# Selecting the top keys in other passes, and one gate projection seven heads later

## The chip, the cores and the metric

The kernel runs on one core of a Trainium2 chip. The metric is the device time of one execution, from launch to the last write, in microseconds (us). TensorE (PE in the rows; PEld is its weight load) does the matrix products, VectorE (DVE) and ScalarE (ACT) the element work, GpSimd (POOL) some of it, and SyncE (SP) issues most transfers.

## The reference, cut to what matters

One decoder block over 1024 positions and 1024 channels. Eight heads of forgetting attention (the fox heads, 0 to 7) and eight heads of sparse attention (the DSA heads, 8 to 15) run on projections of the same normed input; two gates, sigmoids of 1024 projected columns each, weigh the two branches; then come an output projection and an MLP.

```python
iscore = jnp.where(causal[None], iscore, -jnp.inf)
_, sel = lax.top_k(iscore, topk)              # 256 keys per query, one list for all DSA heads
...
merged = (jax.nn.sigmoid(gate_fox) * (y_fox @ w_branch_fox)
          + jax.nn.sigmoid(gate_dsa) * (y_dsa @ w_branch_dsa))
```

The list of 256 keys depends on an index score that is shared by all DSA heads. Ties are broken in favour of the earlier key.

## The kernel before, in words

The queries lie in eight tiles of 128. For tiles 2 to 7 (those with more than 256 admissible keys) the kernel finds the 256th largest score of each query by bisection on its 32 bits, 16 high bits first (`Thi`), then 16 low bits (`Tlo`). One step of `bisect_step` counts, for each query, the keys at or above a candidate: tiles 2 to 5 on VectorE (line 487), tiles 6 and 7 on ScalarE with a sign function and its accumulator (line 484); line 507 takes both counts. Afterwards `select_tile(i)` turns the threshold into a mask: `sel[i]` becomes 0 for a chosen key and 1e30 for the others, W = (i+1)*128 columns wide, so 384 to 1024. `sel[i]` holds the low bits of those keys whose high bits equal the threshold, until then. `bjunk` and `eqt` are one buffer each, so the six tiles take turns in them.

The masks are read first by head 8, the first DSA head, in line 552, behind line 551, which adds a position bias and runs for DSA heads alone.

The heads run in a Python loop. Each turn issues the attention of head n, the q and k projection of head n+1 (`proj_qk`), every second time a v projection, and the gate projections that the table `GC` gives to this turn (`gate_tile`). All these projections go through `gemm_h`: 24 products per half, two halves, in the two PSUM banks of tile `g`, which rotate. A bank is free again when ScalarE and VectorE have copied it out: lines 308 to 314 for q and k (the last VectorE reads are lines 310 and 314), line 598 for a gate. Their weights come through a ring of three staging tiles `st` and two pairs `whi`, `wlo`, so they keep the order of the program among themselves.

In the same turns, four bisection steps are issued behind each fox head, and the six `select_tile` calls behind head 7. The framework then orders the instructions of each engine by a list schedule, and each engine runs its own list strictly in order. The schedule pulls the bisection and the selection forward: in the trace the selection runs beside head 5. In attention, line 552 adds the mask and takes the row minimum from PSUM tile `S`, line 556 is the exponential, line 559 scales by the reciprocal of the sum (558), and lines 573 and 574 split the transposed weights into `ph` and `pl` for the product with V.

Of the kernel before, what the change touches and what calls it, by code (L numbers as in the profile page):

```python
# [16 lines left out]
AF = mybir.ActivationFunctionType  # L17
ALU = mybir.AluOpType
# [14 lines left out]
BIG = 1.0e30  # L33
# [24 lines left out]
def block_kernel(ctx: ExitStack, tc: tile.TileContext, x, c, w_ada, b_ada, g_norm1, w_in, b_forget,  # L58
                 rel_bias, w_bf, w_bd, w_out, g_norm2, w_mlp1, w_mlp2, g_final, onehot, out):
    nc = tc.nc  # L60
# [47 lines left out]
    def split_w(pieces, lo_eng=None, kt=KT, dst=None):  # L108
        st = stg.tile([P, 1024], F32, name="st", tag="st")
        view = st.rearrange("p (k c) -> p k c", k=kt)  # L110
        for d0, d1, src in pieces:
            nc.sync.dma_start(view[:, :, d0:d1], src)
        return split_st(st, lo_eng, dst)
# [47 lines left out]
    isc, sel = [None, None], [None, None]  # L161
# [293 lines left out]
    cnt = pA.tile([P, NQ], F32, name="cnt")  # L455
    goal = pA.tile([P, NQ], F32, name="goal")
    nct = pA.tile([P, NQ], F32, name="nct")
# [52 lines left out]
    def select_tile(i):  # L510
        q, W = i - 2, (i + 1) * P
        hi = isc[i].bitcast(I16)[:, 1::2]
        L = sel[i].bitcast(U16)
        th, tl, nd = Thi[:, q:q + 1], Tlo[:, q:q + 1], need[:, q:q + 1]
        gt, eq = bjunk[:, :W], eqt[:, :W]
        nc.vector.tensor_scalar(gt, L, tl, None, op0=ALU.is_gt, op1=ALU.add, accum_out=cnt[:, q:q + 1])
        nc.vector.tensor_tensor(nd, nd, cnt[:, q:q + 1], op=ALU.subtract)
        nc.vector.tensor_scalar(eq, L, tl, None, op0=ALU.is_equal)
        nc.vector.scalar_tensor_tensor(gt, hi, th, gt, op0=ALU.is_gt, op1=ALU.add)
        nc.vector.scalar_tensor_tensor(eq, hi, th, eq, op0=ALU.is_equal, op1=ALU.mult)  # L520
        nc.vector.tensor_tensor_scan(out=L, data0=eq, data1=eq, initial=0.0, op0=ALU.add, op1=ALU.max)
        nc.vector.scalar_tensor_tensor(eq, L, nd, eq, op0=ALU.is_le, op1=ALU.mult)
        nc.vector.tensor_tensor(gt, gt, eq, op=ALU.add)
        nc.vector.tensor_scalar(sel[i], gt, -BIG, BIG, op0=ALU.mult, op1=ALU.add)


    def attention(kind, h, qk, V, Yd=None):
# [164 lines left out]

    heads = [(k, h) for k in range(2) for h in range(NH)]
    yd_stack, wo_stack = ExitStack(), ExitStack()
    GC = (2, 2, 2, 1, 1, 1, 1, 1, 1, 1, 1, 1, 1)
    GATES, g0 = {}, 0
    for n, w in enumerate(GC):
        GATES[n] = tuple(range(g0, g0 + w))
# [19 lines left out]
    for n, (kind, h) in enumerate(heads):  # L718
# [18 lines left out]
        if n == NH - 1:  # L737
            for i in range(2, NTT):
                select_tile(i)
# [22 lines left out]
    for cp in range(4):  # L762
        hi, lo = split_w([(0, 256, wbv[1][:, :, cp * 256:cp * 256 + 256])], nc.gpsimd, 4)
        hv, lv = hi.rearrange("p (k c) -> p k c", k=4), lo.rearrange("p (k c) -> p k c", k=4)
        for c2 in range(2):
            ct, cs = 2 * cp + c2, slice(c2 * P, c2 * P + P)
            for half in range(2):
                sl = slice(half * 512, half * 512 + 512)
                gt = pY.tile([P, 512], F32, name="gt2", tag="gt2", bufs=3)
# [22 lines left out]
    with ExitStack() as st4:  # L792
# [6 lines left out]
        for ch in range(2):  # L799
# [3 lines left out]
            for t in range(NTT):  # L803
                hf, tl = t // 4, slice((t % 4) * P, (t % 4) * P + P)
# [398 lines left out]
```

## Time and profile before

| | us |
|---|---|
| median of 3 runs | 1657.38 |
| lowest and highest | 1656.96, 1659.05 |
| the profiled execution | 1664.09 |
| its span, first to last instruction | 1662.3 |
| busy: PE, DVE, ACT, POOL | 1582.9, 1155.4, 955.7, 684.4 |
| mean granted TensorE clock | 0.976 |

The rows further down come from the one profiled execution. Times there are counted from the start of its span. A granted clock of 1.00 is 2.4 GHz, of 0.50 it is 1.2 GHz; a mean between them is a stretch that had both. The seven stretches of 198 to 535 are cut at the first exponential of each head: head 1 begins at 198, head 2 at 243, head 7 at 503, and head 8 at 535.

### The profile page before, as it was taken

Reading aid. Unit: us, or ns where it says so; the run is one execution under the profiler, and the core shown is the slowest. Engines: PE = TensorE matmul, PEld = TensorE weight load, DVE = VectorE, ACT = ScalarE, POOL = GpSimd, SP = SyncE. Lnnn points to the kernel's source line nnn. Section 1 sums busy time; section 2 is a strip of 40 time slices with the busy share of each in tenths; the row PEclk is TensorE's granted clock in tenths of the full one; section 3 lists DMA queues with packets and bytes.
Section 4 is the critical chain, followed back from the end, with each engine's and each line's share of the span. In section 5 each row is a group of like instructions: output and inputs, shape, how many; then the busy total and the mean of one; then the engine's idle time right before and its main releaser. Section 6 shows DMA issues by size and latency. Waiting matters only on the chain.

```text
span 1662.3 us, 22793 instructions
## 1 busy us (share of the span) xinstructions
PE 1582.9 (95%) x7585; PEld 1310.5 (79%) x7585; DVE 1155.4 (70%) x2293; ACT 955.7 (57%) x1674; POOL 684.4 (41%) x569
## 2 busy tenths in 40 slices
PE   5989999998989999999999998999999989999998
PEld 3767787786778888888887787888888868888887
DVE  6786999999954556556666535866565464758987
ACT  4366997898566777677753135554555343533433
POOL 3421121221123574756643211677776544334730
PEclk8999999998999999999999999999999989999999
DMA  9221122222232443444876435554444469665862
GB/s 299 77 59 51 50 74 55 52 66 49 74 77 67 125 133 106 131 143 139 287 257 230 151 121 194 168 185 160 154 147 158 178 240 361 230 212 188 281 209 102
DMA packets 221757, 250.92 MB, mean 151 GB/s; under 512 B 49072, under 2 KB 134144, under 8 KB 221640
## 3 DMA queue, kind: packets, MB, share of 16 engines
q1 hardware_dynamic: 215304, 235.83, 44.8%
q10 hardware_dynamic: 6336, 13.63, 2.1%
q8 instruction: 60, 0.98, 0.2%
q14 instruction: 57, 0.47, 0.1%
HBM read 184.38 MB, written 65.03 MB: 150 GB/s over the span
## 4 chain that ended last, share of the span: by engine, by line
PE 74%; DVE 14%; ACT 4%; DMA 4%; issue 3%; POOL 1%; SPq 1%; DVEq 0%; ACTq 0%; POOLq 0%
PE g L75 33%; PE S L75 23%; PE tr L75 8%; PE pv L75 7%; DVE bjunk L487 3%; PE ptr L572 2%; DVE acc L247 1%; DMA gt<-G_d 1%; DVE pl L574 1%; DVE sp L552 1%; DMA wap<-in_w_ada_dram 1%; ACT eqt L484 1%; ACT sp L556 1%; DVE gt L777 1%; ACT sp L559 1%
## 5 line engine op out<-in xcount | busy, mean ns | idle before, releaser
L75 PE MATMUL g<-h_hi,whi 128*128 128x512 f32 x656 | 266.5, 406 | 8.8 <-DVE KA L314 6.4
L75 PE MATMUL g<-h_hi,wlo 128*128 128x512 f32 x656 | 263.9, 402 | 0.0
L75 PE MATMUL g<-h_lo,whi 128*128 128x512 f32 x656 | 263.0, 401 | 0.0
L118 POOL TENSOR_TENSOR wlo<-st,whi 128x1024 fp32r<-128x1024 f32 x56 | 137.3, 2453 | 293.9 <-ACT whi L117 265.4
L1026 DVE TENSOR_TENSOR ut<-rw,ut 128x1024 fp32r<-128x1024 f32 x112 | 179.0, 1644 | 69.5 <-ACT ut L1025 69.5
L1025 ACT ACTIVATE ut<-rw 128x1024 fp32r<-128x1024 f32 x112 | 112.0, 1052 | 144.9 <-PE pv L75 66.5
L1040 POOL TENSOR_TENSOR rw<-rw 128x1024 f32<-128x1024 f32 x40 | 115.6, 2893 | 127.3 <-DMA rw<-in_w_mlp_dram 110.0
L75 PEld LDWEIGHTS g<-h_hi,whi 128*128 128x128 f32 x656 | 126.2, 192 | 34.8 <-DVE KA L314 4.3
L75 PEld LDWEIGHTS g<-h_hi,wlo 128*128 128x128 f32 x656 | 125.6, 191 | 24.7
L75 PEld LDWEIGHTS g<-h_lo,whi 128*128 128x128 f32 x656 | 125.8, 192 | 23.6
L75 PE MATMUL S<-ut 128*128 128x512 f32 (+1 forms) x576 | 138.2, 384 | 0.0
L75 PEld LDWEIGHTS S<-ut 128*128 128x128 f32 x576 | 106.5, 190 | 21.5 <-DVE ut L1026 0.4
L574 DVE TENSOR_TENSOR pl<-ptr,ph 128x512 fp32r<-128x512 f32 (+1 forms) x160 | 99.5, 630 | 27.2 <-ACT ph L573 23.5
L573 ACT ACTIVATE ph<-ptr 128x512 fp32r<-128x512 f32 (+1 forms) x160 | 86.1, 551 | 55.4 <-PE ptr L572 51.2
L556 ACT ACTIVATE sp<-sp,mn 128x128 f32<-128x128 f32 (+7 forms) x128 | 98.5, 771 | 28.3 <-DVE mn L552 28.1
L117 ACT ACTIVATE whi<-st 128x1024 fp32r<-128x1024 f32 x70 | 73.8, 1054 | 65.9 <-PE g L75 23.1
L487 DVE TENSOR_SCALAR_CACHE_REDUCE bjunk<-sel_all,cand 128x384 bf16<-128x384 int16 (+7 forms) x132 | 106.3, 806 | 1.4
L559 ACT ACTIVATE sp<-sp,mn 128x128 f32<-128x128 f32 (+7 forms) x128 | 96.8, 770 | 17.2 <-DVE mn L558 16.7
L75 PE MATMUL g<-ut 128*128 128x512 f32 (+1 forms) x384 | 94.7, 382 | 6.1 <-ACT ut L1025 4.6
L572 PE MATMUL ptr<-ident,sp 128*128 128x128 f32 x576 | 91.2, 274 | 9.8 <-DVE pl L574 9.8
L75 PE MATMUL pv<-ph,V 128*128 128x256 f32 x320 | 86.8, 291 | 1.6 <-DVE yt L581 0.9
L75 PEld LDWEIGHTS g<-ut 128*128 128x128 f32 x384 | 69.9, 191 | 21.0 <-ACT ut L1025 5.0
(433 smaller groups left out, 3883.4 us busy)
## 6 DMA issues: line engine op xcount, KB each, us to landing
rw<-in_w_mlp_dram SPq DMA_DIRECT2D x72, 512.0 KB
rw<-U_d SPq DMA_DIRECT2D x56, 512.0 KB
wap<-in_w_ada_dram SPq DMA_DIRECT2D x64, 256.0 KB
st<-in_w_mlp_dram SPq DMA_DIRECT2D x32, 512.0 KB
st<-in_w_in_dram SPq DMA_DIRECT2D x26, 512.0 KB
U_d<-cc SPq DMA_DIRECT2D x48, 256.0 KB
st<-in_w_in_dram SPq DMA_DIRECT2D x33, 256.0 KB
G_d<-t SPq DMA_DIRECT2D x32, 256.0 KB
```

What stands on the lines that cost most here:

```text
L75: nc.tensor.matmul(o, l, r, start=start, stop=stop)
L117: nc.scalar.activation(hi, st, AF.Copy)
L118: (lo_eng or nc.vector).tensor_tensor(lo, st, hi.bitcast(F32), op=ALU.subtract)
L487: nc.vector.tensor_scalar(bjunk[:, :(i + 1) * P], sel[i].bitcast(dt), thr[:, q], None, op0=ALU.is_ge, op1=ALU.add, accum_out=cnt[:, q])
L556: nc.scalar.activation(sp[:, :W], sp[:, :W], AF.Exp, bias=mn[:, len(cs) - 1:len(cs)], scale=-1.0, accum_out=mn[:, 2:3])
L559: nc.scalar.activation(sp[:, :W], sp[:, :W], AF.Copy, scale=mn[:, 3:4])
L572: nc.tensor.transpose(tr[:, n * P:(n + 1) * P], pt[s][:, kb * P:(kb + 1) * P], ident)
L573: nc.scalar.activation(ph[:, z:], tr[:, z:], AF.Copy)
L574: nc.vector.tensor_tensor(pl[:, z:], tr[:, z:], ph[:, z:].bitcast(F32), op=ALU.subtract)
L1025: nc.scalar.activation(ut[:, n], t, AF.Copy)
L1026: nc.vector.tensor_tensor(ut[:, n + 1], t, ut[:, n].bitcast(F32), op=ALU.subtract)
L1040: nc.gpsimd.tensor_tensor(o, a, b, op=op)
```

## The change

Two edits. In `select_tile`, the count of keys above the threshold moves from a VectorE pass with accumulator to a ScalarE sign pass with accumulator, whose result is +1 or -1 (so `cnt` is twice the number less W, which two one-column instructions make good); the sum `gt + eq` and the final scaling are replaced by one VectorE pass that gives 0 for chosen and 1 for other keys, and a ScalarE copy that scales it by 1e30. And in the table of gates, turn 1 issues one gate projection in place of two, and turn 7 two in place of one; the gates between keep their order, so each turn from 2 to 6 does the gate of one number lower.

```diff
--- before.py
+++ after.py
@@ -513,15 +513,18 @@
         L = sel[i].bitcast(U16)
         th, tl, nd = Thi[:, q:q + 1], Tlo[:, q:q + 1], need[:, q:q + 1]
         gt, eq = bjunk[:, :W], eqt[:, :W]
-        nc.vector.tensor_scalar(gt, L, tl, None, op0=ALU.is_gt, op1=ALU.add, accum_out=cnt[:, q:q + 1])
-        nc.vector.tensor_tensor(nd, nd, cnt[:, q:q + 1], op=ALU.subtract)
+        nt, nw = nct[:, q:q + 1], goal[:, q:q + 1]
+        nc.vector.tensor_scalar(nt, tl, -1.0, -0.5, op0=ALU.mult, op1=ALU.add)
+        nc.vector.tensor_scalar(nw, nd, float(W // 2), None, op0=ALU.subtract)
+        nc.scalar.activation(gt, L, AF.Sign, bias=nt, accum_out=cnt[:, q:q + 1])
         nc.vector.tensor_scalar(eq, L, tl, None, op0=ALU.is_equal)
-        nc.vector.scalar_tensor_tensor(gt, hi, th, gt, op0=ALU.is_gt, op1=ALU.add)
         nc.vector.scalar_tensor_tensor(eq, hi, th, eq, op0=ALU.is_equal, op1=ALU.mult)
         nc.vector.tensor_tensor_scan(out=L, data0=eq, data1=eq, initial=0.0, op0=ALU.add, op1=ALU.max)
+        nc.vector.scalar_tensor_tensor(nd, cnt[:, q:q + 1], -0.5, nw, op0=ALU.mult, op1=ALU.add)
+        nc.vector.scalar_tensor_tensor(gt, hi, th, gt, op0=ALU.is_gt, op1=ALU.add)
         nc.vector.scalar_tensor_tensor(eq, L, nd, eq, op0=ALU.is_le, op1=ALU.mult)
-        nc.vector.tensor_tensor(gt, gt, eq, op=ALU.add)
-        nc.vector.tensor_scalar(sel[i], gt, -BIG, BIG, op0=ALU.mult, op1=ALU.add)
+        nc.vector.scalar_tensor_tensor(gt, eq, -1.0, gt, op0=ALU.mult, op1=ALU.is_gt)
+        nc.scalar.activation(sel[i], gt, AF.Copy, scale=BIG)
 
 
     def attention(kind, h, qk, V, Yd=None):
@@ -692,7 +695,7 @@
 
     heads = [(k, h) for k in range(2) for h in range(NH)]
     yd_stack, wo_stack = ExitStack(), ExitStack()
-    GC = (2, 2, 2, 1, 1, 1, 1, 1, 1, 1, 1, 1, 1)
+    GC = (2, 1, 2, 1, 1, 1, 1, 2, 1, 1, 1, 1, 1)
     GATES, g0 = {}, 0
     for n, w in enumerate(GC):
         GATES[n] = tuple(range(g0, g0 + w))
```

The first place is VectorE's list for one tile of the selection, the one of 640 columns. Before (`bjunk` is `gt`, `eqt` is `eq`, rows of `pl`, `yt` and `yl` belong to the attention):

```order
L518 TENSOR_SCALAR eqt<-sel_all,Tlo 128x640
L516 TENSOR_SCALAR bjunk,cnt<-sel_all,Tlo 128x640
L520 SCALAR_TENSOR_TENSOR eqt<-isc,Thi,eqt 128x640
L517 TENSOR_TENSOR need<-need,cnt 128x1
L519 SCALAR_TENSOR_TENSOR bjunk<-isc,Thi,bjunk 128x640
L574 TENSOR_TENSOR pl<-ptr,ph 128x512
L581 TENSOR_TENSOR yt<-pv,yt 64x256
L521 SCALAR_TENSOR_TENSOR sel_all<-eqt 128x640
L574 TENSOR_TENSOR pl<-ptr,ph 128x512
L588 TENSOR_TENSOR yl<-yt,yh 64x256
L522 SCALAR_TENSOR_TENSOR eqt<-sel_all,need,eqt 128x640
L523 TENSOR_TENSOR bjunk<-bjunk,eqt 128x640
```

The same tile after the change, where lines are three higher behind the edit (555 is the mask line 552, `goal` is `nw`):

```order
L520 TENSOR_SCALAR eqt<-sel_all,Tlo 128x640
L523 SCALAR_TENSOR_TENSOR need<-cnt,goal 128x1
L524 SCALAR_TENSOR_TENSOR bjunk<-isc,Thi,bjunk 128x640
L521 SCALAR_TENSOR_TENSOR eqt<-isc,Thi,eqt 128x640
L522 SCALAR_TENSOR_TENSOR sel_all<-eqt 128x640
L525 SCALAR_TENSOR_TENSOR eqt<-sel_all,need,eqt 128x640
L555 ISA sp,mn<-S,cmask 128x384
L555 ISA mn 128x1
L555 ISA sp,mn<-S,cmask 128x512
L555 ISA mn 128x1
L526 SCALAR_TENSOR_TENSOR bjunk<-eqt,bjunk 128x640
```

Line 524 of before ends the tile one row further down. The count is gone from VectorE's list; line 523, which takes ScalarE's count, stands right behind the first comparison, and the reading of `bjunk` by ScalarE stands between the tiles.

The second place is VectorE where the q and k projection of head 6 is copied out (`QB`, `KA`). Before, from the end of the bisection on:

```order
L508 SCALAR_TENSOR_TENSOR Tlo<-cnt,Tlo 128x6
L516 TENSOR_SCALAR bjunk,cnt<-sel_all,Tlo 128x384
L518 TENSOR_SCALAR eqt<-sel_all,Tlo 128x384
L310 SCALAR_TENSOR_TENSOR QB<-g,QA 64x512
L517 TENSOR_TENSOR need<-need,cnt 128x1
L519 SCALAR_TENSOR_TENSOR bjunk<-isc,Thi,bjunk 128x384
L520 SCALAR_TENSOR_TENSOR eqt<-isc,Thi,eqt 128x384
L310 SCALAR_TENSOR_TENSOR QB<-g,QA 64x512
L558 RECIPROCAL mn<-mn 128x1
L521 SCALAR_TENSOR_TENSOR sel_all<-eqt 128x384
L574 TENSOR_TENSOR pl<-ptr,ph 128x512
L581 TENSOR_TENSOR yt<-pv,yt 64x256
```

The two rows of line 314 follow nine and eleven rows behind this piece. After the change both rows of line 310 stand three rows ahead of this piece:

```order
L561 RECIPROCAL mn<-mn 128x1
L505 TENSOR_SCALAR cand<-Tlo 128x6
L480 TENSOR_SCALAR nct<-cand 128x2
L487 TENSOR_SCALAR bjunk,cnt<-sel_all,cand 128x384
L487 TENSOR_SCALAR bjunk,cnt<-sel_all,cand 128x512
L487 TENSOR_SCALAR bjunk,cnt<-sel_all,cand 128x640
L561 RECIPROCAL mn<-mn 128x1
L487 TENSOR_SCALAR bjunk,cnt<-sel_all,cand 128x768
L584 TENSOR_TENSOR yt<-pv,yt 64x256
L314 TENSOR_TENSOR KA<-g,KA 64x512 x2
L577 TENSOR_TENSOR pl<-ptr,ph 128x512 x2
L591 TENSOR_TENSOR yl<-yt,yh 64x256
```

Here the last bisection step stands between lines 310 and 314, and the selection's passes begin behind both.

The third place is SyncE's queue around turn 1. A load of `st` in one piece of 128 columns is for a gate or a v projection, two pieces of 64 are for q and k. Before:

```order
L112 DMA st<-in_w_in_dram 128x8x128
L599 DMA G_d<-t_2189 128x512
L590 DMA Y_d<-yh 64x256
L590 DMA Y_d<-yl 64x256
L599 DMA G_d<-t_2217 128x512
L112 DMA st<-in_w_in_dram 128x8x64 x2
L302 DMA QB<-E_d 4x1024
L303 DMA KB<-E_d 4x1024
L590 DMA Y_d<-yh 64x256
L590 DMA Y_d<-yl 64x256
L599 DMA G_d<-t_2251 128x512
```

After:

```order
L112 DMA st<-in_w_in_dram 128x8x64 x2
L602 DMA G_d<-t_2189 128x512
L593 DMA Y_d<-yh 64x256
L593 DMA Y_d<-yl 64x256
L602 DMA G_d<-t_2217 128x512
L112 DMA st<-in_w_in_dram 128x8x128
L302 DMA QB<-E_d 4x1024
L303 DMA KB<-E_d 4x1024
L593 DMA Y_d<-yh 64x256
L593 DMA Y_d<-yl 64x256
L593 DMA Y_d<-yh 64x256
```

The load of head 3's q and k weights has moved ahead of where the second gate's stood, and the store of that gate's first half (the last row of before) is issued later. Around turn 7 the same load and the two stores come in addition.

## Rows read from the trace of the kernel before

**Rows 1.** The page, part 1: busy time and share of each engine.

```profile
PE 1582.9 (95%) x7585; PEld 1310.5 (79%) x7585; DVE 1155.4 (70%) x2293; ACT 955.7 (57%) x1674; POOL 684.4 (41%) x569
```

**Rows 2.** Windows, one per fox head: start:end, length, busy times (instructions), clock, DMA.

```profile
198.00:243.00 45.00, 44.53 (x239) 38.00 (x238) 41.35 (x133) 41.51 (x83) 8.62 (x11) 1.00 0.27 73
243.00:306.00 63.00, 60.52 (x298) 50.76 (x297) 58.49 (x168) 50.61 (x98) 9.46 (x11) 0.95 0.22 60
306.00:356.00 50.00, 47.12 (x246) 39.16 (x245) 46.55 (x147) 44.94 (x88) 12.93 (x44) 1.00 0.22 57
356.00:406.00 50.00, 42.29 (x206) 34.94 (x206) 46.67 (x144) 45.07 (x90) 8.75 (x13) 0.90 0.25 61
406.00:461.00 55.00, 51.53 (x259) 41.58 (x258) 53.62 (x101) 29.43 (x58) 8.48 (x11) 1.00 0.20 59
461.00:503.00 42.00, 37.11 (x195) 30.98 (x194) 21.03 (x61) 29.39 (x60) 6.23 (x10) 0.96 0.30 75
503.00:535.00 32.00, 32.00 (x179) 27.62 (x179) 13.83 (x42) 20.84 (x42) 9.20 (x12) 1.00 0.20 55
```

**Rows 3.** Timeline of TensorE, 390 to 402: start, length, instruction, idle time before.

```profile
396.51 0.34 PE L75 MATMUL S<-KB,QB 68*128 68x384 f32 x1
400.81 0.90 PE L572 MATMUL ptr<-ident,sp 128*128 128x128 f32 x3 [3.96 <-DVE pl L574]
```

**Rows 4.** Timeline of VectorE, 390 to 460.

```profile
396.07 0.61 DVE L516 TENSOR_SCALAR_CACHE_REDUCE bjunk<-sel_all,Tlo 128x384 bf16<-128x384 uint16 x1
...
399.24 0.93 DVE L521 TENSOR_TENSOR_SCAN sel_all<-eqt 128x384 uint16<-128x384 bf16 x1
400.09 0.66 DVE L574 TENSOR_TENSOR pl<-ptr,ph 128x512 fp32r<-128x512 f32 x1
...
404.14 0.69 DVE L314 TENSOR_TENSOR KA<-g,KA 64x512 fp32r<-64x512 f32 x1
...
452.87 0.67 DVE L310 SCALAR_TENSOR_TENSOR QB<-g,QA 64x512 fp32r<-64x512 f32 x1
...
454.40 0.40 DVE L524 TENSOR_SCALAR sel_all<-bjunk 128x1024 bf16<-128x1024 bf16 x1
```

**Rows 5.** Line 551, whose first instruction opens the first DSA head.

```profile
L551 DVE TENSOR_TENSOR S<-S,toep x64: 284/426/433, 535.1 to 851.0; 128x256 f32<-128x256 f32 x56, 128x128 f32<-128x128 f32 x8
```

**Rows 6.** Lines of VectorE from 390 to 460: group, count, busy, mean ns, idle before.

```profile
L516 DVE TENSOR_SCALAR_CACHE_REDUCE bjunk<-sel_all,Tlo 128x384 bf16<-128x384 uint16 (+5 forms) x6 | 5.6, 938 | 0.0
L522 DVE SCALAR_TENSOR_TENSOR eqt<-sel_all,need,eqt 128x384 bf16<-128x384 uint16 (+5 forms) x6 | 5.6, 937 | 0.0
...
L523 DVE TENSOR_TENSOR bjunk<-bjunk,eqt 128x384 bf16<-128x384 bf16 (+5 forms) x6 | 3.1, 510 | 0.1
...
L518 DVE TENSOR_SCALAR eqt<-sel_all,Tlo 128x384 bf16<-128x384 uint16 (+5 forms) x6 | 2.4, 397 | 0.0
...
L524 DVE TENSOR_SCALAR sel_all<-bjunk 128x384 bf16<-128x384 bf16 (+5 forms) x6 | 2.0, 337 | 0.1
...
L517 DVE TENSOR_TENSOR need<-need,cnt 128x1 f32<-128x1 f32 x6 | 0.9, 146 | 0.0
L516 DVE DVE_READ_ACCUMULATOR bjunk<-sel_all,Tlo 128x1 f32 x6 | 0.5, 81 | 0.0
```

**Rows 7.** Timeline of TensorE inside one projection, 420 to 425.

```profile
420.18 0.40 PE L75 MATMUL g<-h_hi,whi 128*128 128x512 f32 x1
...
424.54 0.39 PE L75 MATMUL g<-h_lo,whi 128*128 128x512 f32 x1
```

**Rows 8.** Lines by shape, whole span: ScalarE's sign counts and scaled copies.

```profile
L484 ACT ACTIVATE eqt<-sel_all,nct 128x1024 bf16<-128x1024 uint16 x16 | 18.2, 1139 | 0.1
...
L484 ACT ACTIVATION_READ_ACCUMULATOR eqt<-sel_all,nct 128x1 f32 x66 | 12.5, 189 | 0.0
...
L559 ACT ACTIVATE sp<-sp,mn 128x384 f32<-128x384 f32 x16 | 9.7, 608 | 1.5 <-DVE mn L558 1.5
```

**Rows 9.** Lines, whole span: VectorE's step that waits for ScalarE's counts.

```profile
L507 DVE TENSOR_TENSOR cnt<-cnt,goal 128x6 f32<-128x6 f32 x32 | 9.6, 300 | 6.4 <-ACT eqt L484 5.6
```

## Prediction

> **What bounds the kernel now.** The page's first part says TensorE: busy for 95% of the span [rows 1]. That is a mean over stages, so the next view is a table of windows, one for each fox head [rows 2], and it shows two regimes. In heads 1 to 5 (198 to 461, 263 us) VectorE is the fullest engine, busy for 246.7 us or 94%, and in head 5 for 53.62 of 55. TensorE is idle there for 17.0 us (length less busy time, added over five rows), most of it, 7.7 us, in head 4, where its granted clock also falls to 0.90, a mean of stretches at 2.4 and at 1.2 GHz, which costs another 0.10 x 42.3 = 4.2 us. From head 7 on it turns: TensorE is busy for all 32.00 of 32 us at full clock and VectorE for 13.83.
>
> Third, the timeline inside the worst hole [rows 3]. TensorE finishes a score product that began at 396.51 and begins nothing until 400.81; for 3.96 us of that it waits for line 574. VectorE is not late with that line because the line is long: it began the selection of the first tile at 396.07, was still in its scan at 399.24, and came to 574 at 400.09 [rows 4]. Nothing else could run on TensorE, since both projection banks were held by the q and k of head 6, whose last copy, line 314, ran at 404.14. So the reader should see an in-order VectorE list in which selection stands in front of what TensorE waits for.
>
> Fourth, who needs the selection? Its last pass is at 454.40 [rows 4], and the first DSA head begins at 535.1 [rows 5]. The mask is ready 80 us early. No wait for the mask can therefore be shortened; only the load on VectorE in heads 1 to 5 counts.
>
> **The change, VectorE.** Over six tiles it removes the count with its accumulator reading (5.6 + 0.5 us), the one-column subtraction (0.9), the sum (3.1) and the scaling (2.0): 12.1 us [rows 6]. It adds one scalar-tensor-tensor pass of full width, which is what line 522 is: 5.6 us. And it adds three one-column instructions per tile, 18 in all. Line 517 is the same size at 0.146 us [rows 6]: 2.6 us. Net 12.1 - 5.6 - 2.6 = 3.9 us less. The small ones are the uncertain part: at the 0.300 us of line 507 [rows 9] they are 5.4 us and the saving is 1.1; if they slipped into gaps at no cost it would be 6.5. I take 3.9, because line 517 is the nearest row.
>
> **ScalarE.** It gains a sign pass, an accumulator reading and a copy per tile. Signs go from 0.61 us for 384 columns (the scaled copy of that width, as the nearest row) to 1.139 for 1024 [rows 8], so 6 x 0.87 = 5.2; readings 6 x 0.189 = 1.1; copies again 5.2: 11.5 us. Head 5's window has 29.43 us of ScalarE work in 55 [rows 2], so by capacity it fits. The Trainium skill speaks against it: "ScalarE: Activation LUTs", section "Rules for kernel authors", gives element multiplication to VectorE, as up to three times faster in bf16. The trace agrees on the ratio: the last pass is 2.0 us on VectorE [rows 6] against 5.2 here. If ScalarE were the engine waited for, the sum would grow by 5.2; by the window it is not.
>
> **A wait is added.** Line 523 of the change takes ScalarE's count on VectorE, and behind it, in order, stand the rest of the tile and the attention's lines 552 and 574, for which TensorE waits. As `bjunk` is one buffer, ScalarE must first copy the tile before out of it. Copy, sign and reading are 0.87 + 0.87 + 0.19 = 1.93 us. Cover is what VectorE has ahead of line 523: in some tiles the comparison, a masked product and the scan, but in the tile of 640 columns, as the order shows, only the comparison, 0.40 us [rows 6]. Bounds: five hand-overs at nothing hidden and the first sign are 5 x 1.93 + 0.8 = 10.5 us. At the other end, line 507 is the same kind of wait now and costs 5.6 us over 32 steps [rows 9], 0.18 each, so 0.9 us for five. I take 0.9, since the schedule places other work there as it does ahead of line 507.
>
> **The moved gate.** One gate is 48 products of 512 columns. From 420.18 to 424.54 there are nineteen steps of one product each [rows 7]: 0.229 us, so 11.0 us of TensorE. Its weight load, split and two stores move along with it; SyncE issues the same number, and GpSimd, busy 9.20 of 32 in head 7 [rows 2], has room. In head 7 TensorE has no idle time, so the gate costs its full 11.0 us there. What comes back in heads 1 to 5 is the question.
>
> A landmark helps: the copy of head 7's q and k, line 310 at 452.87 [rows 4]. Before, all that VectorE then still has of the selection is the pass of 0.40 us at 454.40. After, in the order, the last pass of the sixth tile and all of the seventh stand behind it: five passes like 522 at 0.937 x 1024/704 = 1.36 or less, a scan at 0.93 x 1024/384 = 2.5 [rows 4, 6] and a comparison of 0.5, together near 9.8; part of each pass is fixed and doesn't grow with the width, so I take 9. Up to the landmark VectorE thus has 3.9 + 9 - 0.4 = 12.5 us less, and with the hand-over waits 11.6 us less. If it stays busy for 94%, the stretch shortens by 11.6/0.94 = 12.4 us. Judged by TensorE alone, with its waits unchanged, it would be 11.0. The two engines agree within 1.4 us, and I take VectorE's, the fuller one.
>
> The 9 us behind the landmark fall into head 6, where VectorE is busy for 21.03 of 42 [rows 2]: nothing. Without that cover they would be up to 9 us.
>
> **Sum.** 11.0 - 12.4 = -1.4 us. The profiled execution took 1664.09 us, 0.4% above the median of 1657.38; 1662.7 of it, scaled to the median, is **1656.0**. I hold 0.2%, 3.3 us, to be what a measurement can tell from no change, so this is no change: **0.43**. Its own range, with the small instructions between their bounds (-2.6 to +2.8, over 0.94), is 1653 to 1659.
>
> **Rival 1, the hole in head 4 closes (faster).** After the change VectorE copies head 6's q and k behind the last bisection steps and ahead of the selection, with 574 directly behind them. What stood in front of 574, 4.0 us and most of it selection [rows 4], is then gone, with the wait of 3.96 and the fall of the clock behind it, 4.2: up to 8.2 us, or 1647.9; half of it is 1651.9. For it: the order. Against it: both banks are still held together, with four counting passes between lines 310 and 314, and with one gate less there is less to fill such a hole in heads 2 to 4. It shows from 2 us on: **0.36**.
>
> **Rival 2, VectorE waits for ScalarE (slower).** Place: line 523. If all 10.5 us are exposed, that is 9.6 more than in the sum, over 0.94: 1666; half of that, 1661. It decides from about 5.3 us of wait in the stretch. For it: in heads 1 to 4 ScalarE is busy for 88% [rows 2], and its list is in order too. Against it: in head 5 it has room. The rule cited above, of the Trainium skill's page "ScalarE: Activation LUTs", points this way. **0.13**.
>
> **Rival 3, the gate is not given back.** If VectorE's list keeps its pairing of selection with heads, the stretch shortens by 3.9/0.94 = 4.1 and head 7 pays 11.0: +6.9, 1664.3. It decides where the stretch shortens by less than 7.7. Against it stands the order, in which the selection ends later relative to the heads. **0.08**.
>
> **Numbers.** Faster 0.36 from rival 1, same 0.43, slower 0.13 + 0.08 = 0.21. The range reaches into rival 1 to 1648, its full price, and into rival 2 to 1662.5; left out are the far part of rival 2 and rival 3, and a little below.
>
> **What would show it.** Right: about 8.6 us of scalar-tensor-tensor and one-column time against 12.1 removed; head 7's copy 11 to 13 us earlier than 452.87; head 7 some 11 us longer, with TensorE full; idle time of VectorE at line 523 under 2 us in all. Rival 1: no wait of 4 us at 574 near the copy of head 6's q and k, and a clock near 1.00 in head 4. Rival 2: VectorE idle at 523 or 526 for 5 us and more. Wrong altogether would be a gain or loss behind head 8, where the change touches only the order of a schedule; I count nothing for it.

## The result, and the profile after it

The changed kernel is slower: 1669.24 us median of six runs (1664.95 to 1672.40) against 1657.85 for the kernel before in the same comparison, a ratio of 1.0065 with a 95% interval of 1.0048 to 1.0083. The forecast was 1656.0, and its range ended at 1662.5. The profiled execution took 1672.40 us, with a span of 1670.6.

TensorE's total, in the page's part 1, shows nothing: it was busy for 1582.9 us before [rows 1], and the products are the same.

```profile
PE 1582.7 (95%) x7585; PEld 1310.2 (78%) x7585; DVE 1156.6 (69%) x2287; ACT 965.0 (58%) x1692; POOL 686.4 (41%) x569
```

The windows by head, cut as in [rows 2] at the first exponential of each head (columns: start:end, length, busy times of PE, PEld, DVE, ACT and POOL, clock, DMA share, GB/s), from head 1 to head 7:

```profile
196.40:244.20 47.80, 47.43 (x252) 40.34 (x251) 43.08 (x137) 43.39 (x86) 8.57 (x11) 1.00 0.23 58
244.20:298.40 54.20, 49.99 (x253) 42.01 (x252) 49.78 (x145) 44.71 (x88) 8.55 (x11) 0.97 0.21 57
298.40:347.20 48.80, 45.77 (x243) 38.66 (x242) 44.30 (x139) 44.63 (x86) 12.99 (x44) 0.99 0.25 65
347.20:402.70 55.50, 47.27 (x223) 39.32 (x222) 51.23 (x164) 48.87 (x97) 6.43 (x12) 0.85 0.22 53
402.70:450.10 47.40, 43.45 (x217) 35.71 (x216) 46.90 (x95) 34.52 (x67) 9.80 (x11) 0.95 0.15 43
450.10:497.40 47.30, 41.70 (x212) 34.77 (x211) 27.60 (x67) 32.20 (x66) 6.21 (x10) 0.91 0.32 90
497.40:543.10 45.70, 45.70 (x252) 39.34 (x252) 19.23 (x52) 27.45 (x55) 15.70 (x20) 1.00 0.33 91
```

Heads 1 to 6 together took 305 us before [rows 2] and 301.0 now. Head 7 took 32 and takes 45.7. So the moved gate is paid for in head 7, as forecast, and only about 4 us are given back ahead of it, which was not.

Where the time goes can be read from these rows with one measure, used from here on: TensorE's waste in a window is its idle time (length less busy time) and what the lower clock costs (one less the clock, times the busy time). In head 4 that is 55.50 - 47.27 = 8.2 and 0.15 x 47.27 = 7.1. Over the seven heads it was 30.6 us [rows 2] and is 40.4; head 4 went from 11.9 to 15.3, head 5 from 3.5 to 6.1, head 6 from 6.4 to 9.4. The 9.8 us more are the 9.7 by which the seven heads grew (337.0 from head 1's start to the first DSA row before, 346.7 now), since the rest of the windows, TensorE's work at the full clock, is the same: 306.4 before and 306.3 now. The first DSA row has moved from 535.1 [rows 5] to 543.1, while head 1 began 1.6 us earlier:

```profile
L554 DVE TENSOR_TENSOR S<-S,toep x64: 277/425/433, 543.1 to 864.5; 128x256 f32<-128x256 f32 x56, 128x128 f32<-128x128 f32 x8
```

The timeline of TensorE shows the holes (start, length, instruction, idle time before it):

```profile
380.56 0.80 PE L75 MATMUL S<-KA,QA 128*128 128x512 f32 x1 [2.63 <-DVE mn L555]
...
392.79 0.79 PE L75 MATMUL g<-h_hi,whi 128*128 128x512 f32 x1 [4.77 <-DVE KA L314]
393.38 0.63 PE L75 MATMUL g<-h_lo,whi 128*128 128x512 f32 x1
393.81 0.63 PE L75 MATMUL g<-h_hi,wlo 128*128 128x512 f32 x1
...
445.14 1.07 PE L575 MATMUL ptr<-ident,sp 128*128 128x128 f32 x4 [2.59 <-DVE pl L577]
...
448.30 0.63 PE L75 MATMUL g<-h_hi,whi 128*128 128x512 f32 x1
448.73 0.63 PE L75 MATMUL g<-h_lo,whi 128*128 128x512 f32 x1
...
492.03 0.90 PE L575 MATMUL ptr<-ident,sp 128*128 128x128 f32 x3 [4.12 <-DVE pl L577]
```

In place of the wait of 3.96 us [rows 3] stands one of 4.77 ahead of a projection product: both projection banks are held by head 6's q and k until line 314. Behind the holes at 392.79 and 445.14 the products start 0.43 us apart instead of 0.229 [rows 7], which is about half the rate, 1.2 GHz for 2.4; the granted clock over 440 to 450 is 0.77. Of the 40.4 us of waste, 15.0 are such lost clock. The Trainium skill, "TensorE: Matmul & The Clock Gate", section "HAM oscillation — how this bites in real kernels", tells of a kernel whose batches of matmuls each start at the lower rate, because a wait for data has come between them. The rows behind the hole of 4.77 us agree, with 0.43 us between products; here a wait of 2.59 us has the same behind it.

VectorE around the landmark (line 310, at 452.87 before [rows 4]), and the end of the selection:

```profile
441.35 1.14 DVE L525 SCALAR_TENSOR_TENSOR eqt<-sel_all,need,eqt 128x896 bf16<-128x896 uint16 x1
442.42 0.68 DVE L310 SCALAR_TENSOR_TENSOR QB<-g,QA 64x512 fp32r<-64x512 f32 x1
...
443.35 1.08 DVE L526 SCALAR_TENSOR_TENSOR bjunk<-eqt,bjunk 128x896 bf16<-128x896 bf16 x1
...
444.42 1.26 DVE L577 TENSOR_TENSOR pl<-ptr,ph 128x512 fp32r<-128x512 f32 x2
...
459.19 1.21 DVE L526 SCALAR_TENSOR_TENSOR bjunk<-eqt,bjunk 128x1024 bf16<-128x1024 bf16 x1
```

The new selection itself, VectorE's and ScalarE's lines from 370 to 500 (busy, mean ns, idle before):

```profile
L522 DVE TENSOR_TENSOR_SCAN sel_all<-eqt 128x384 uint16<-128x384 bf16 (+5 forms) x6 | 9.7, 1619 | 0.7 <-ACT bjunk L519 0.6
...
L525 DVE SCALAR_TENSOR_TENSOR eqt<-sel_all,need,eqt 128x384 bf16<-128x384 uint16 (+5 forms) x6 | 6.7, 1124 | 0.0
...
L526 DVE SCALAR_TENSOR_TENSOR bjunk<-eqt,bjunk 128x384 bf16<-128x384 bf16 (+5 forms) x6 | 5.3, 877 | 0.0
L523 DVE SCALAR_TENSOR_TENSOR need<-cnt,goal 128x1 f32<-128x1 f32 x6 | 3.0, 503 | 0.0
```

```profile
L519 ACT ACTIVATE bjunk<-sel_all,nct 128x384 bf16<-128x384 uint16 (+5 forms) x6 | 5.3, 879 | 0.1
L527 ACT ACTIVATE sel_all<-bjunk 128x384 bf16<-128x384 bf16 (+5 forms) x6 | 4.7, 787 | 2.1 <-DVE bjunk L526 2.1
L519 ACT ACTIVATION_READ_ACCUMULATOR bjunk<-sel_all,nct 128x1 f32 x6 | 1.1, 187 | 0.0
```

VectorE waits 0.6 us in all for ScalarE's sign pass, ahead of the scan of line 522, which overwrites what that pass reads, and nothing ahead of line 523, which takes the count. One row of line 523 lasts 2.29 us, from 410.17, which is no hidden wait, for ScalarE had read that count out by 409.00:

```profile
408.81 0.19 ACT L519 ACTIVATION_READ_ACCUMULATOR bjunk<-sel_all,nct 128x1 f32 x1
```

Rival 2 did not happen.

### The profile page after: what moved, and what is told of

It reads as the page before. It is cut to its first block, busy times and chain, and to the rows that moved or that the text cites. A ratio compares the mean times of both kernels' runs of the same rounds, so it can differ in the third digit from the quotient of the medians.

```text
span 1670.6 us, 22820 instructions
## 1 busy us (share of the span) xinstructions
PE 1582.7 (95%) x7585; PEld 1310.2 (78%) x7585; DVE 1156.6 (69%) x2287; ACT 965.0 (58%) x1692; POOL 686.4 (41%) x569
## 4 chain that ended last, share of the span: by engine, by line
PE 71%; DVE 14%; DMA 5%; ACT 4%; issue 3%; POOL 2%; SPq 1%; DVEq 0%; ACTq 0%; POOLq 0%
PE g L75 32%; PE S L75 21%; PE tr L75 8%; PE pv L75 7%; PE ptr L575 2%; DVE bjunk L487 2%; DVE acc L247 2%; DVE ut L1029 1%; DMA wap<-in_w_ada_dram 1%; DVE sp L555 1%; DMA t<-G_d 1%; DMA gt<-G_d 1%; DVE pl L577 1%; ACT eqt L484 1%; POOL wap L618 1%
## 5 line engine op out<-in xcount | busy, mean ns | idle before, releaser
L562 ACT ACTIVATE sp<-sp,mn 128x128 f32<-128x128 f32 (+7 forms) x128 | 96.4, 769 | 13.9 <-DVE mn L561 13.5
```

The source lines that it names most:

```text
L562: nc.scalar.activation(sp[:, :W], sp[:, :W], AF.Copy, scale=mn[:, 3:4])
```

## Experiments

Theory A was formed on these two traces: the gate is work that fills TensorE where it would wait, so its price depends on where it stands. Theory B blames the new selection's passes, which stand beside the hole at 445.14. Theory C is that any edit re-draws the order and shifts waste by some us. (In the expectations heads are counted from one: the second is head 1 of the rows, the fifth head 4, the eighth head 7.)

All results in one table. The numbers of "before" are medians of the runs beside each set (1660.52 for e1 to e4, 1659.18 for e5 to e8, 1659.91 for e9 to e12). "Heads 1-7" is the length from head 1's start to the first DSA row in each profiled execution, and the waste is by the formula above, in all and in heads 4, 5 and 6. These lengths repeat: the changed kernel has 346.7 and 346.9 in two executions, and heads 1 to 6 have 304.8 us before and 304.5 in e4, which does not touch them.

| kernel | median us | ratio to before (95%) | heads 1-7 | waste | heads 4, 5, 6 |
|---|---|---|---|---|---|
| before (profiled) | 1657.85 | 1 | 337.0 | 30.6 | 11.9, 3.5, 6.4 |
| changed | 1669.24 | 1.0065 (1.0048-1.0083) | 346.7 | 40.4 | 15.3, 6.1, 9.4 |
| e1 gate alone | 1667.00 | 1.0035 (1.0022-1.0048) | 347.5 | 40.9 | 15.6, 6.1, 8.9 |
| e2 selection alone | 1656.61 | 0.9975 (0.9964-0.9986) | 335.0 | 26.6 | 10.2, 4.7, 4.6 |
| e3 gate from head 7 to 4 | 1646.66 | 0.9920 (0.9901-0.9939) | 326.5 | 13.8 | 4.6, 2.1, 0.6 |
| e4 one gate more in head 7 | 1672.95 | 1.0075 (1.0056-1.0094) | 349.7 | 28.9 | 11.9, 3.5, 6.4 |
| e5 no gate 3 in head 1 | 1657.40 | 0.9985 (0.9975-0.9995) | 332.4 | 39.5 | 14.8, 7.3, 8.9 |
| e6 changed, gate to head 4 | 1650.31 | 0.9944 (0.9928-0.9960) | 326.5 | 19.6 | 1.2, 0.6, 8.3 |
| e7 changed again | 1670.64 | 1.0063 (1.0048-1.0078) | 346.9 | 41.7 | 15.5, 6.1, 9.3 |
| e8 selection, gate from 7 to 4 | 1645.11 | 0.9919 (0.9904-0.9934) | 323.5 | 14.2 | 5.0, 3.0, 0.1 |
| e9 changed, early gate loads | 1668.53 | 1.0045 (1.0028-1.0062) | 344.2 | 39.2 | 14.7, 6.2, 9.8 |
| e10 selection, two gates pulled | 1644.01 | 0.9906 (0.9890-0.9922) | 323.9 | 13.1 | 5.0, 1.5, 0.0 |
| e11 changed, gate to head 6 | 1659.15 | 0.9993 (0.9981-1.0006) | 335.4 | 32.9 | 15.4, 6.2, 1.7 |
| e12 e8 with early gate loads | 1647.01 | 0.9915 (0.9898-0.9932) | 323.8 | 14.4 | 5.6, 2.5, 0.2 |

**e1, the gate alone.** The old selection with the changed table of gates:

```
-    GC = (2, 2, 2, 1, 1, 1, 1, 1, 1, 1, 1, 1, 1)
+    GC = (2, 1, 2, 1, 1, 1, 1, 2, 1, 1, 1, 1, 1)
```

> The old selection, with the gate moved from the second to the eighth head. Theory A (the gate was filling in the heads that VectorE bounds, and is dear where TensorE is full): the seventh and eighth heads pay 11 us more, the heads before them give back only a part of 11, so this kernel carries most of the loss: 6 to 11 us slower than before, with the windows of the first six heads less than 6 us shorter in sum. Theory B (the new selection's order opens the new holes beside the copy of the seventh head's q and k): the gate is given back almost whole, the time is within 3 us of before. Theory C (any edit re-draws the order, and the waste of TensorE moves by some us either way): anything from -5 to +11, and no additivity with the next kernel.

6.5 us slower by medians. In the heads it is the changed kernel over again: 305.1 us for heads 1 to 6 (304.8 before, cut the same way), so nothing is given back, and 42.4 for head 7. Head 5, where the passes of theory B would do their harm, has the changed kernel's 6.1 us of waste with the old selection too. Heads 4 to 7, windows as above:

```profile
348.40:405.20 56.80, 48.49 (x227) 40.33 (x226) 52.18 (x163) 48.85 (x96) 6.43 (x12) 0.85 0.22 52
405.20:453.70 48.50, 43.71 (x219) 35.38 (x218) 48.26 (x98) 27.84 (x54) 9.22 (x11) 0.97 0.15 42
453.70:503.40 49.70, 43.89 (x225) 36.09 (x224) 29.62 (x70) 30.04 (x61) 6.22 (x10) 0.93 0.32 89
503.40:545.80 42.40, 42.40 (x234) 36.46 (x233) 19.59 (x53) 26.93 (x56) 17.86 (x22) 1.00 0.35 101
```

**e2, the selection alone.** The changed kernel with the first line of that table restored.

> The new selection, with the gates where they stood. Theory A: the VectorE work that is saved (3.9 us) lies in heads where VectorE is the bound, so 0 to 4 us faster than before, and never slower by over 3. Theory B: 6 to 11 us slower, with the stall of TensorE beside the copy of the seventh head's q and k as in the changed kernel. Theory C: anything from -5 to +8; the sum of this and of the gate-only kernel then differs from +11 by several us.

3.9 us faster, so theory B falls. VectorE's selection lines (370 to 500, all groups added up) took 42.2 us before and 38.3 here, which is the forecast saving of 3.9. In the changed kernel they took 41.2, in the main since a one-column instruction and a full pass were stretched there (3.0 us for line 523 above, 0.8 here; 6.7 for line 525, 5.6 here). Two of the lines, and TensorE's wait for `pl` that was 3.96 us before:

```profile
L525 DVE SCALAR_TENSOR_TENSOR eqt<-sel_all,need,eqt 128x384 bf16<-128x384 uint16 (+5 forms) x6 | 5.6, 936 | 0.0
...
L523 DVE SCALAR_TENSOR_TENSOR need<-cnt,goal 128x1 f32<-128x1 f32 x6 | 0.8, 131 | 0.0
```

```profile
398.04 0.90 PE L575 MATMUL ptr<-ident,sp 128*128 128x128 f32 x3 [2.56 <-DVE pl L577]
```

**e3, a gate moved the other way**, from head 7 into head 4, with the old selection:

```
+    GC = (2, 2, 2, 1, 2, 1, 1, 0, 1, 1, 1, 1, 1)
```

> The old selection, with one gate moved the other way: from the eighth head, where TensorE has no idle time, to the fifth, where TensorE lost 11.9 us by holes and half clock. Theory A: the eighth head gives back its 11 us and the fifth takes 0 to 8 of them, so 3 to 11 us faster than before. Theory B says nothing of the gates, by it the gate costs its 11 us wherever it stands: within 3 us of before. Theory C: -8 to +5, whatever the place.

13.9 us faster, more than any theory had said. Head 7 gives back only 3.5 us (28.7 against 32.2): 75 products into `g` run there where 92 did, so that most of the gate's 48 have been replaced by others from behind. The heads that took the gate become shorter as well: 297.8 us for heads 1 to 6 against 304.8, although they hold the gate's products in addition. Heads 4 to 7, with the clock at or near 1.00 throughout:

```profile
353.30:406.00 52.70, 48.10 (x253) 40.18 (x252) 48.65 (x147) 45.42 (x90) 9.76 (x14) 1.00 0.27 68
406.00:455.90 49.90, 49.23 (x246) 40.49 (x245) 49.33 (x96) 28.48 (x56) 7.52 (x11) 0.97 0.28 72
455.90:495.50 39.60, 39.05 (x212) 33.24 (x212) 22.01 (x62) 31.40 (x63) 7.48 (x11) 1.00 0.28 72
495.50:524.20 28.70, 28.70 (x165) 24.92 (x164) 16.71 (x46) 21.07 (x44) 7.87 (x13) 1.00 0.24 62
```

**e4, one gate more in head 7**: `GATES[7] += (0,)` behind the loop over the table.

> One gate more than before: gate 0 is computed a second time in the eighth head (the same values are stored twice). It prices a gate in a head where TensorE is full. Theory A and B: 11 us slower than before (66 products at 0.229 us is 11.0 with 48 of them counted, so 10 to 12), all of it in the eighth head. Theory C: 5 to 17.

12.4 us slower, just above the 10 to 12 of theory A, and the waste of heads 1 to 6 is about that of before; head 7 grows from 32.2 to 45.2 us. The forecast 11.0 for a gate in a full head is right to about 1.5. (A gate is 48 products; the 66 in the expectation is a slip.)

```profile
500.40:545.60 45.20, 45.20 (x250) 38.87 (x250) 18.74 (x52) 27.69 (x55) 17.69 (x21) 1.00 0.32 92
```

**e5, the gate in head 1 left out**: the function that computes a gate stores zeros from GpSimd for gate 3.

```
+        if g == 3:
...
+                nc.gpsimd.memset(e, 0.0)
+                nc.sync.dma_start(G_d[g, :, half * 512:half * 512 + 512], e)
...
+            return
```

> The kernel before without the products of gate 3, the second gate of the second head: its output is stored as zeros from GpSimd, so the result leaves out that gate. It prices the gate where the change took it away. Theory A (the gate filled idle TensorE time there): 3 to 8 us faster than before, about the 12.4 us of the extra gate in the eighth head less the 5.8 us that the moved gate cost. The prediction's own step (the gate is given back whole, 11 us): 10 to 13 us faster.

Only 1.8 us by medians, 0.15% by the ratio, less than any theory had said. The products are gone (48 x 0.229 = 11.0 us) and TensorE's waste is 8.9 us higher instead, in heads 4 to 6, whose rows are close to those of e1, with nothing in head 7 to pay for it:

```profile
343.60:399.40 55.80, 46.60 (x224) 38.94 (x224) 52.17 (x163) 49.01 (x97) 6.42 (x12) 0.88 0.22 53
399.40:447.90 48.50, 43.83 (x218) 35.72 (x217) 48.26 (x98) 27.86 (x55) 9.24 (x11) 0.94 0.15 42
447.90:497.80 49.90, 44.09 (x226) 36.29 (x225) 29.63 (x70) 30.05 (x62) 6.21 (x10) 0.93 0.34 88
```

**e6, the changed kernel with the gate in head 4 instead of head 7**: `GC = (2, 1, 2, 1, 2, 1, 1, 1, 1, 1, 1, 1, 1)`.

> The changed kernel with the gate moved from the second head to the fifth instead of the eighth. Theory A (the place it goes to is what is dear): the eighth head is as before, so -6 to +3 us against before, and 8 to 14 us faster than the changed kernel. If the loss came of taking the gate out of the second head, it would stay: over 5 us slower than before.

8.9 us faster than before and 20.3 faster than the changed kernel of the same set, for one gate in another head. Both are more than theory A had said. TensorE in the stretch where the changed kernel waited for line 314:

```profile
390.62 0.39 PE L75 MATMUL g<-h_hi,wlo 128*128 128x512 f32 x1
...
393.16 0.50 PE L75 MATMUL g<-h_hi,whi 128*128 128x512 f32 x1
```

And ScalarE's copies of the two halves of head 6's q, in the changed kernel:

```profile
381.39 0.59 ACT L308 ACTIVATE QA<-g 64x512 fp32r<-64x512 f32 x1
...
382.61 0.59 ACT L308 ACTIVATE QA<-g 64x512 fp32r<-64x512 f32 x1
```

In e6:

```profile
385.91 0.58 ACT L308 ACTIVATE QA<-g 64x512 fp32r<-64x512 f32 x1
...
395.73 0.59 ACT L308 ACTIVATE QA<-g 64x512 fp32r<-64x512 f32 x1
```

Without the gate the two halves end 1.2 us apart and hold both banks together; with it they are 9.8 us apart, one bank goes on with projection products while VectorE still counts, and TensorE has no hole.

**e7, the changed kernel once more**, beside e5, e6 and e8.

> The changed kernel once more, beside the others on one chip. If the two parts add up: +1 to +3 us on before (5.8 for the gate less 4.1 for the selection). If there is an interaction, the new selection loses its gain once the gate stands in the eighth head: +8 to +13 us as in the first timing.

The first timing is confirmed. In time the two parts do not add up: 6.5 - 3.9 = 2.6 us by e1 and e2, for 11.5 here. In the heads they nearly do: 10.5 - 2.0 = 8.5 us, for 9.9. So most of what is missing lies outside of heads 1 to 7.

**e8, the selection with e3's table.**

> The new selection with a gate moved the other way, from the eighth head to the fifth. If the parts add up: 17 to 18 us faster than before (13.3 and 4.1). If the two compete for the same holes of TensorE: 11 to 15 us faster.

14.1 us faster, no more than e3 alone, by times that agree within their intervals: where the gate already fills the holes, the selection's 3.9 us of VectorE buy nothing that the time shows, though heads 1 to 7 are 3.0 us shorter than in e3.

**e9, early loads of the gates**, on the changed kernel: in the branch step both stored gate tiles are loaded ahead of the weights' conversion. It concerns the part behind heads 1 to 7. There TensorE waits at the line that combines a gate with its projection, and that line for the gate's load: 7.2 us over five waits in the changed kernel from 560 to 1010, 2.0 before, and e1's list of waits has none at that line.

```
+        gl = []
+        for c2 in range(2):
+            gl.append(pQ.tile([P, 512], F32, name="t512", tag="t512", bufs=3))
+            nc.sync.dma_start(gl[c2], G_d[2 * cp + c2, :, sl])
         hi, lo = split_w(...)
...
-            g = pQ.tile([P, 512], F32, name="t512", tag="t512", bufs=3)
-            nc.sync.dma_start(g, G_d[ct, :, sl])
+            g = gl[c2]
```

> The changed kernel with one thing moved: in the branch step, the loads of the two stored gate tiles are written ahead of the weights' conversion instead of inside the loop over the columns. TensorE's order stays as in the changed kernel, only the sync queue's is different. If the loss has a second part behind the first eight heads (TensorE waits 7.2 us on the line that combines a gate with its projection, which waits for the gate's load; 2.0 in the kernel before): 2 to 5 us faster than the changed kernel, so 5 to 9 us slower than before. If that wait is covered or moves to another load: as the changed kernel, 10 to 11 us slower than before.

8.6 us slower than before; the interval overlaps with the changed kernel's, and the wait stayed at 5.7. The first row is the changed kernel's, the second e9's (waits of TensorE: total, times, longest):

```profile
PE g L75 <- DVE t L660: 7.2, 5, 1.9
```

```profile
PE g L75 <- DVE t L663: 5.7, 4, 1.8
```

The edit did not take the wait away, so this test settles nothing.

**e10, two gates pulled forward**: `GC = (2, 2, 2, 1, 2, 2, 1, 0, 0, 1, 1, 1, 1)` with the new selection.

> The new selection and two gates pulled forward: one from the eighth head to the fifth, one from the ninth to the sixth. Theory A in its sharper form (a gate gains only what it finds of waste where it goes): with the first gate moved, TensorE's waste in the sixth and seventh heads is 2.9 us, so the second gate gains 0 to 4 us on the kernel with one gate pulled: 13 to 18 us faster than before. If a gate were worth its 11 us wherever VectorE bounds: 24 us faster than before.

15.9 us faster, which e8's interval doesn't tell apart; both beat the kernel before and the changed one. Once the waste of heads 5 and 6 is 3.1 us, a second gate there has little to fill.

**e11, the changed kernel with the gate in head 6**: `GC = (2, 1, 2, 1, 1, 1, 2, 1, 1, 1, 1, 1, 1)`.

> The changed kernel with the gate moved from the second head to the seventh instead of the eighth. Theory A: the seventh head has 9 us of waste in the changed kernel, but that of the fifth head (14.6) stays open: between the fifth head as the goal (-9.3 us against before) and the eighth (+10.5), at -5 to +5 us. If only the distance to the eighth head counted and the seventh is as full: +8 to +12.

No different from before that can be measured, and 0.7% faster than the changed kernel by the two ratios. Only head 6's waste is filled (9.4 to 1.7), and head 4's stays. With e3 and e6 this leaves little room for theory C within the heads: a gate went twice into head 4 and once into head 6, and each time the waste of its head shrinks most (in e3 head 6's goes from 6.4 to 0.6 as well, in e6 head 5's from 6.1 to 0.6):

```profile
347.80:403.40 55.60, 47.29 (x223) 39.38 (x222) 51.27 (x164) 48.91 (x97) 6.43 (x12) 0.85 0.21 53
...
450.80:501.90 51.10, 50.41 (x267) 42.93 (x266) 27.09 (x66) 33.30 (x66) 7.75 (x11) 0.98 0.34 96
```

**e12, e8 with the early loads of e9.**

> The new selection, one gate pulled from the eighth head to the fifth, and the early loads of the gate tiles. Where the pulled order already has few waits at the line that combines them, nothing is left to win: 12 to 15 us faster than before, as without the early loads. If every order pays for the late loads: 15 to 18 us faster.

12.9 us faster, as e8 within the intervals.

## Why the prediction was wrong

**The step that failed** is "The 9 us behind the landmark fall into head 6, where VectorE is busy for 21.03 of 42 [rows 2]: nothing", with the one that it rests on, that the copy of head 7's q and k measures how far the stretch has come. The copy did come earlier, by 10.5 us (442.42 for 452.87), 8.9 of them behind head 1's start. But by head 7's start only 3.8 were left, and in e1 a copy 6.4 us earlier behind head 1's start (446.81, head 1 at 198.3) left none. The stretch from the copy to head 7's start, before and after:

```profile
452.87:502.80 49.93, 43.51 (x225) 35.77 (x225) 27.87 (x73) 37.19 (x73) 8.64 (x11) 0.97 0.26 65
442.42:497.40 54.98, 46.15 (x223) 37.83 (x223) 35.22 (x81) 39.79 (x78) 8.58 (x11) 0.88 0.28 80
```

It is 5.1 us longer, where the prediction had nothing. VectorE has 7.4 us more to do there (35.22 for 27.87), not far from the 9 that it had put there, and TensorE's waste is 14.4 us for 7.7. The copy had been put earlier among the rest; the work put behind it was still to be done, in a stretch whose engines have room in the mean and where TensorE waits for VectorE all the same. The hole of 2.59 us at 445.14 was one of 1.24 before. The one of 4.12 at 492.03 is not of the change, for it was 4.10 before:

```profile
454.19 0.55 PE L572 MATMUL ptr<-ident,sp 128*128 128x128 f32 x3 [1.24 <-DVE pl L574]
...
497.44 0.55 PE L572 MATMUL ptr<-ident,sp 128*128 128x128 f32 x3 [4.10 <-DVE pl L574]
```

A landmark shows progress only when the same work lies behind it in both kernels.

**Under it lay a wrong picture of heads 1 to 5.** The prediction took VectorE for the bound, since it is busy for 94%, and asked how much of its load is gone. By that, adding work for TensorE there could at best cost nothing. e3 and e6 show that it gains. The prediction's own rows did not single VectorE out: TensorE was busy for 246.0 of the same 263 us, VectorE for 246.7 [rows 2]. Its check by TensorE, 11.0 us "with its waits unchanged", failed as well, for the waste grew by 9.8. Neither engine's sum sets these heads; their hand-overs do, and projection products are what TensorE does while it waits. e5 shows it in the other direction: 11.0 us of TensorE's work taken out of head 1 come back as 8.9 us of waste in heads 4 to 6.

**Right:** head 7 pays in full (forecast 11.0 us, 12.4 by e4, 13.5 in the window of the changed kernel, which also takes work left over). VectorE's saving of 3.9 us is met in e2, in part by luck: the terms themselves give 12.1 - 5.3 - 1.9 = 4.9 there (5.3 us for line 526, 1.9 for the one-column lines), and passes that were stretched in one kernel or the other take 1 us back. (The sign of "about 8.6 us" is 5.6 + 2.6 = 8.2 by the prediction's own terms, and head 4's 7.7 of 17.0 us of idle time are the largest part, but not most of it; neither slip enters the sum.) ScalarE's 11.5 us measured 5.3 + 4.7 + 1.1 = 11.1. The Trainium skill's rule for element multiplication ("ScalarE: Activation LUTs", section "Rules for kernel authors") agrees in its ratio, 4.7 us for the last pass against 2.0 [rows 6]. The selection alone is faster all the same; ScalarE had room there (29.43 of 55 us in head 5 [rows 2]).

**The rivals.** Rival 3 was the right one in kind, at a chance of 0.08: heads 1 to 6 shorten by 3.8 us where it gave the stretch 4.1, and the gate is not given back. Its time of 1664.3 is short of 1669.2 by 2.5 us more in head 7 (13.5 for 11.0) and by what is behind the heads. Its reason did not hold: VectorE's pairing did change, since the copy came 8.9 us earlier behind head 1's start, and what was missing was filler for TensorE. That 3.8 lies so near to 4.1 is not shown to be more than luck. Rival 1's hole did not close, it grew, for the cause named against it: both banks are held together, and there is one gate less to fill it. In e2, where the gate stays, it shrinks to 2.56 us. The counting passes between lines 310 and 314 are not the last: the trace has four more of line 487 behind 314, from 397.15 to 400.5, so the last bisection step but one stands there, where the section on the change says the last. Rival 2 is refuted by 0.6 us.

**What stays open.** "I count nothing" for the part behind head 8 was wrong by some us. The changed kernel and e1 lose about the same in the heads (9.7 and 10.5 us), but end 11.4 and 6.5 us behind by medians. The waits for the stored gates (7.2 us against none) lie at a fitting place and have about the right size. But e9 failed to remove them, and e4 has 6.3 us of them and yet loses no more in all (12.4 us) than in its heads (12.7):

```profile
PE g L75 <- DVE t L657: 6.3, 5, 1.9
```

So the cause is argued and not shown. For the same reason the parts close to a few us only: by e4 and e5 the moved gate should cost 12.4 - 1.8 = 10.6 us, and e1 measured 6.5.

## What to carry to other kernels

Independent TensorE work is a resource: before moving a piece of it, measure TensorE's waste (idle time and lost clock) by stage, and price the piece as its length less the waste that it fills where it goes, plus the waste that it leaves open where it stood, which may show up several stages later. Here one gate more cost 12.4 us in a head without waste, and the kernels that had one moved into head 4, where two banks were held together, were 8.9 to 15.9 us faster than before (15.9 with a second gate moved into head 5). Such a price is good to a few us (by e4 and e5 it is 10.6 for the moved gate, which cost 6.5 in e1). An engine that is busy for 94% is no proof of a bound: look at the other engines' share and at their holes beside it, which here showed that the hand-overs set the pace.

## What the runs showed of the hardware

The lost clock was two thirds of the damage in the heads: of the 9.8 us of added waste, 6.3 are products at the lower rate behind holes (8.7 us before, 15.0 after) and 3.5 idle time. A hole of 2.59 us at 445.14 was followed by products 0.43 us apart. And single VectorE instructions are stretched now and then: line 523, of one column, has one instance of 2.29 us among six that are otherwise 0.15. It is nothing of the change: the kernel before has one of 2.33 us at line 505, where others take 0.17. Why is not shown.
